# Stick-breaking attention: who copies the meta-token weights and the second half of the split keys

## The chip, the cores and the metric

The kernel runs on one core of a Trainium2 chip. The metric is the device time of one execution in microseconds (us), lower is better; a profile of a single execution of the kernel before the change stands beside it. The engines are called PE (TensorE matmul), PEld (its weight load), DVE (VectorE), ACT (ScalarE), POOL (GpSimd) and SP (SyncE, which here issues nearly all DMAs).

## The reference, cut to what matters

One layer of a decoder trunk: a normalised input goes through one wide projection into gated retention (4 heads) and stick-breaking attention (16 heads of 64), both are gated, merged, projected, and followed by a SwiGLU FFN. 512 tokens have 16 learned meta tokens put before them, so a row of keys is 528 long. The change lies in the attention alone:

```python
z = jnp.einsum('bhtd,bhsd->bhts', q_blk, k_pre) * scale
valid = (s_pos[None, :] < t_pos[:, None]) & (s_pos[None, :] >= PAD)
log_not = jnp.where(valid, jax.nn.log_sigmoid(-z), 0.0)
after = lax.cumsum(log_not, axis=3, reverse=True) - log_not
a = jnp.where(valid, jnp.exp(jax.nn.log_sigmoid(z) + after), 0.0)
outs.append(jnp.einsum('bhts,bhse->bhte', a, v_pre))
```

The weight of key s for token t is the sigmoid of the score times the product of the complementary sigmoids of all later keys. The first 16 of the 528 columns of the weights `a` belong to the meta tokens.

## The kernel before, in words

All operands of matmuls are split: a value is kept as a hi part, rounded to the matmul's type (fp32r), and a lo part, the rest. Three matmuls (hi by hi, hi by lo, lo by hi) stand for one product. `split` (line 99) makes the hi part on ACT (`activation(..., Copy)`) and the lo part on DVE (`lo_of`, line 96: a subtraction). Weights come from device memory through `load_units` (DMA at line 107 into one of two buffers `raw`, then `split` into `wh` and `wl`, five buffers each).

**The attention stage** works on 8 pairs of heads (two heads of 64 rows fill 128 partitions). For each pair:

- `qk_work` adds two pieces of work for the *next* pair: `q_steps` and `k_steps`. The score matmul contracts over 128 rows: for head 0 the query operand `qa` holds the hi rows above the lo rows, and the key operand `ka` holds the hi rows of k twice, rows 0:64 and again 64:128, so that one matmul gives hi by hi and lo by hi. Head 1 has the mirror image in `qb` and `kb`. A second matmul adds the key's lo part (`kl0`, `kl1`, with zeros in the unused half). `k_steps` makes the keys in two halves of 264 columns; for each half four ACT copies (lines 523 to 526) read the PSUM bank `pk`: `ka` hi, `ka` again into the other rows, `kb` hi, `kb` again; then two DVE subtractions (`kl`, line 96) make the lo parts and release the bank. There are two such banks (`bank_p`), which the projections of the stage share.
- `score` (line 594): two matmuls into a two-bank PSUM tile, two sigmoids on ACT (lines 616 and 618), a reversed running product on DVE (`sm`, line 620) and a product on DVE (`sp`, line 621) give the weights of one head and one block of 128 tokens.
- `turn_meta` (line 624): the 16 meta columns of the four blocks of a head have to be turned, so that keys lie on partitions. POOL copies each block's 16 columns with rounding (hi part, line 629), POOL subtracts (lo part, line 630), DVE transposes the 128x128 tile in 32x32 blocks into `x` (line 631), and four POOL copies (line 634) move the four groups of 32 rows of `x` into 32 rows of one tile, `am`: head 0 in rows 0:32, head 1 in rows 32:64. The whole tile is called `both`.
- `turn` (line 636): PE transposes the other columns into PSUM (`pb`, line 93), `split` makes `ah` and `al`.
- `values` (line 646): the output of a head; the first of its matmuls takes `both` (`pb<-am,vm`), the others `ah` and `al`. ACT (line 655) and DVE (line 656) take the result out of PSUM into `ysb`. The matmul with `both` reads the rows of both heads; those of the other head meet zero weights.

**Order.** `pair` writes out by hand in which order these are called: scores of head 0, a part of the transposes, scores of head 1 in between, `tm` (`turn_meta`) of head 0 at place 10, `pv` (`values`) of head 0 at place 13, `tm` of head 1 at place 17, `pv` of head 1 at place 19, the last. Between the calls `merge` puts matmuls of the projections (next pair's q and k, values, gates) by hand-set shares. In this stage the PE's order is pinned to that program order (`keep_in_program_order`). The orders of ACT, DVE, POOL and SP are mostly chosen when the program is built, by a scheduler that simulates a timeline; the POOL work of `Tokens.row_steps` (line 170, sums of token quarters, six steps behind each `tm` of pairs 1 to 5) is pinned as well. Each engine then runs its queue strictly in order, and so does SP with the DMAs it issues. `k_steps` of a pair is followed in the PE's order by a gate's or the values' projection before the next pair begins; only the first pair's keys are made directly ahead of it.

Tiles that matter here: `ka` one buffer, `kb` two, `mg` (the tile that is transposed) one, `x` one (shared with the values' tail), `am` one, the PSUM banks `bank_p` two and `bank_b` two.

Of the kernel before, what the change touches and what calls it, by code (L numbers as in the profile page):

```python
# [10 lines left out]
F32 = mybir.dt.float32  # L11
F32R = mybir.dt.float32r
AF = mybir.ActivationFunctionType
# [4 lines left out]
NM = 16  # L18
# [16 lines left out]
def hybrid_block(  # L35
# [18 lines left out]
    nc = tc.nc  # L54
    x, out = x[0], out[0]
# [9 lines left out]
    def bank_p():  # L65
        return ps_p.tile([P, 512], F32, tag="p", name="pp")
# [28 lines left out]
    def lo_of(lo, src, hi):  # L95
        nc.vector.tensor_tensor(lo, src, hi.bitcast(F32), op=ALU.subtract)  # L96
# [19 lines left out]
    def feat_units(src, kn=KD):  # L116

        cn = src.shape[1]
        return load_units(src, kn, cn, [(0, kn, c, P) for c in range(0, cn, P)])
# [269 lines left out]
    def feat_steps(dst, unit, xh, xl, kn=KD):  # L389
        wh, wl = unit  # L390
        for k in range(kn):
            mm(dst, wh[:, k, :], xh(k), start=(k == 0), stop=False)
            mm(dst, wh[:, k, :], xl(k), start=False, stop=False)
            mm(dst, wl[:, k, :], xh(k), start=False, stop=(k == kn - 1))
            yield 3 * xh(k).shape[-1]
# [12 lines left out]
    with tc.tile_pool(name="s2", bufs=2, side=RS, reuse_waits="tile") as s2:  # L408
# [88 lines left out]
        def qk_work(work, p):  # L497
            def q_load():
                return feat_units(w_in[:, O_SQ + P * p : O_SQ + P * (p + 1)])

            def q_steps(us):
                ps = bank_p()
                yield from feat_steps(ps, us[0], xtok, ltok)
                qa = s2.tile([P, T], F32R, tag="qa", name="qa", bufs=1)
                qb = s2.tile([P, T], F32R, tag="qb", name="qb")
                nc.scalar.activation(qa[0:64], ps[0:64], AF.Copy)
                nc.scalar.activation(qb[64:128], ps[64:128], AF.Copy)
                lo_of(qa[64:128], ps[0:64], qa[0:64])
                lo_of(qb[0:64], ps[64:128], qb[64:128])
                qks[p] = [(qa, qb)]  # L510

            def k_load():
                return feat_units(w_in[:, O_SK + P * p : O_SK + P * (p + 1)])

            def k_steps(us):
                ka = s2.tile([P, 2, 264], F32R, tag="ka", name="ka", bufs=1)
                kb = s2.tile([P, 2, 264], F32R, tag="kb", name="kb")
                kl1 = kl1s[p % 2]
                for i in range(2):
                    cs = slice(264 * i, 264 * (i + 1))  # L520
                    pk = bank_p()[:, :264]
                    yield from feat_steps(pk, us[0], lambda k: hT[:, k, cs], lambda k: hL[:, k, cs])
                    nc.scalar.activation(ka[0:64, i], pk[0:64], AF.Copy)
                    nc.scalar.activation(ka[64:128, i], pk[0:64], AF.Copy)
                    nc.scalar.activation(kb[64:128, i], pk[64:128], AF.Copy)
                    nc.scalar.activation(kb[0:64, i], pk[64:128], AF.Copy)
                    lo_of(kl0[0:64, i], pk[0:64], ka[0:64, i])
                    lo_of(kl1[64:128, i], pk[64:128], kb[64:128, i])
                qks[p] += [(flat(ka), flat(kb)), (flat(kl0), flat(kl1))]

            work.add(q_load, q_steps)
            work.add(k_load, k_steps)

        s3_pool = []
# [89 lines left out]
        def turn_meta(hd, att):  # L624

            g = s2.tile([P, NT, 32], F32R, tag="mg", name="mg", bufs=1)
            x = s2.tile([P, NT, 32], F32, tag="vs", name="x", bufs=1)
            for i in range(NT):
                nc.gpsimd.tensor_copy(g[:, i, 0:NM], att[i][:, 0:NM])  # L629
                nc.gpsimd.tensor_tensor(g[:, i, NM:], att[i][:, 0:NM], g[:, i, 0:NM].bitcast(F32), op=ALU.subtract)  # L630
            nc.vector.transpose(x.rearrange("p a b -> p (a b)"), g.rearrange("p a b -> p (a b)").bitcast(F32))
            am = ams[hd].rearrange("p (i b r) -> p i b r", i=NT, b=4)
            for b in range(4):
                nc.gpsimd.tensor_copy(am[:, :, b, :], x[32 * b : 32 * (b + 1)])

        def turn(j, att):
            w = T - j * P
# [26 lines left out]
        def pair(p):  # L664
# [9 lines left out]
            def tm(hd, j):  # L674
                turn_meta(hd, att[hd])

                if 1 <= p < 6:
                    for _ in range(6):
                        next(token_sums, None)
# [623 lines left out]
```

## Time and profile before

| | us |
|---|---|
| median of 3 runs | 1223.07 (1222.41 to 1224.04) |
| the profiled execution | 1223.93 |
| its span | 1222.2 |
| PE busy in the span | 1173.2 |
| DVE, ACT, POOL busy | 875.8, 534.0, 381.2 |
| start to 59 us (input norm, values, first q and k): PE busy | 48.70 of 59 |
| 59 to 300 us (the pairs): PE, DVE, ACT, POOL busy | 221.45, 203.06, 154.02, 142.41 of 241 |
| 300 us to the end (retention, output projection, FFN): PE busy | 903.08 of 922 |

How to read it: PE is nearly always busy, and matmul ends are modelled, so what can be won without fewer matmuls is the time in which PE waits. A group's row names the line, the engine, the operation, output and input tiles, the number of instructions, their busy time and the mean of one in ns, then the idle time of the engine before them and what ended it. A line of the view of waits names the engine and line that waited, what it waited for, the total, the number of times and the longest. Timeline rows start with the start and the duration in us. The granted TensorE clock was 1.00 in the pairs' stage. DMA rows give the time from issue to landing.

### The profile page before, as it was taken

To read this page: it belongs to the slowest core of one execution; us is meant where nothing else is said; L and a number is where in the kernel's file an instruction comes from. 1 tells how busy PE (TensorE), PEld (TensorE's weight loads), DVE (VectorE), ACT (ScalarE), POOL (GpSimd) and SP (SyncE) were. 2 spreads that over 40 slices of the span, in tenths; PEclk is the share of its full clock that TensorE was granted. 3 is DMA by queue.
4 is the path that set the end of the run, shared out by engine and by line. 5 is a ranking of instruction groups with operands and counts; after the bars stand their busy time and mean duration, and the time that the engine had idled before them with its cause. 6 is when DMAs were issued, how large, how long until landed. Compare 5 with 4: busy or idle time off the path is not lost.

```text
span 1222.2 us, 18904 instructions
## 1 busy us (share of the span) xinstructions
PE 1173.2 (96%) x7629; PEld 1064.6 (87%) x7629; DVE 875.8 (72%) x1138; ACT 534.0 (44%) x873; POOL 381.2 (31%) x422
## 2 busy tenths in 40 slices
PE   7999998889999999989999999999999999999997
PEld 6888888788889988988898889778899999998886
DVE  6588888887537885586678747776889999984333
ACT  5476666655424434333332424334464444443221
POOL 2037767554033220230213030000256666630000
PEclk9999999999999999999999999999999999999999
DMA  6331111114643214122421424424223333343211
GB/s 192 87 95 44 53 52 56 49 44 144 222 139 110 70 45 137 35 80 71 134 70 45 138 69 121 143 107 155 70 70 105 104 104 104 105 163 130 85 53 69
DMA packets 94503, 118.25 MB, mean 97 GB/s; under 512 B 2488, under 2 KB 71104, under 8 KB 94416
## 3 DMA queue, kind: packets, MB, share of 16 engines
q1 hardware_dynamic: 93984, 115.98, 29.0%
q8 instruction: 60, 0.98, 0.3%
q10 hardware_dynamic: 432, 1.07, 0.3%
q14 instruction: 27, 0.22, 0.1%
HBM read 109.96 MB, written 7.08 MB: 96 GB/s over the span
## 4 chain that ended last, share of the span: by engine, by line
PE 74%; DVE 12%; ACT 3%; POOL 2%; DMA 2%; issue 2%; DVEq 0%; POOLq 0%; ACTq 0%; SPq 0%
PE pp L90 31%; PE pb L90 20%; PE pa L90 18%; PE pc L90 4%; DVE wl L96 2%; DVE sm L620 2%; PE pb L93 2%; DVE sp L621 2%; DVE sl L96 1%; ACT wh L99 1%; POOL mg L629 1%; DMA raw<-in_w_in_dram 1%; DVE kl L96 1%; DMA raw<-in_w_sb_out_dram 1%; POOL mg L630 1%
## 5 line engine op out<-in xcount | busy, mean ns | idle before, releaser
L96 DVE TENSOR_TENSOR wl<-raw,wh 128x1024 fp32r<-128x1024 f32 (+1 forms) x202 | 274.0, 1365 | 81.3 <-ACT wh L99 78.1
L99 ACT ACTIVATE wh<-raw 128x1024 fp32r<-128x1024 f32 (+1 forms) x202 | 201.4, 1007 | 261.3 <-PE pa L90 85.5
L90 PE MATMUL pp<-hT,wh 128*128 128x512 f32 (+2 forms) x308 | 108.7, 353 | 12.9 <-DVE qb L96 7.9
L90 PE MATMUL pp<-hL,wh 128*128 128x512 f32 (+2 forms) x308 | 103.5, 336 | 0.0
L90 PE MATMUL pp<-hT,wl 128*128 128x512 f32 (+2 forms) x308 | 103.4, 336 | 0.0
L96 DVE TENSOR_TENSOR wl<-st,wh 128x1024 fp32r<-128x1024 f32 x54 | 81.0, 1505 | 9.5 <-ACT wh L99 9.5
L90 PE MATMUL pp<-qk,wh 128*128 128x512 f32 x256 | 83.2, 399 | 2.0 <-ACT qk L99 1.7
L90 PE MATMUL pp<-wh,hT 128*128 128x256 f32 (+1 forms) x240 | 77.1, 322 | 2.5 <-DVE kl L96 1.8
L90 PE MATMUL pp<-wh,hL 128*128 128x256 f32 (+1 forms) x240 | 75.3, 314 | 0.8 <-DVE ss L142 0.8
L90 PEld LDWEIGHTS pp<-hT,wh 128*128 128x128 f32 x308 | 58.1, 189 | 20.2 <-issue 9.0
L90 PE MATMUL pp<-wl,hT 128*128 128x256 f32 (+1 forms) x240 | 75.1, 313 | 0.0
L99 ACT ACTIVATE wh<-st 128x1024 fp32r<-128x1024 f32 x54 | 56.0, 1055 | 35.5 <-POOL st L254 17.1
L252 POOL TENSOR_TENSOR st<-raw 128x1024 f32<-128x1024 f32 x7 | 17.2, 2461 | 166.8 <-DMA raw<-in_w_in_dram 166.8
L143 POOL TENSOR_TENSOR rs<-rs,nhalf 128x1 f32<-128x1 f32 x20 | 12.7, 634 | 181.2 <-DVE rs L142 181.2
L629 POOL CAST mg<-sp 128x16 fp32r<-128x16 f32 x64 | 31.1, 487 | 109.5 <-DVE sp L621 53.6
L90 PEld LDWEIGHTS pp<-hT,wl 128*128 128x128 f32 x308 | 58.0, 188 | 6.2
L90 PE MATMUL pa<-hL,wh 128*128 128x264 f32 (+1 forms) x192 | 61.6, 321 | 0.0
L620 DVE TENSOR_TENSOR_SCAN sm<-sm,mask 128x528 f32<-128x528 f32 (+1 forms) x64 | 59.7, 945 | 2.6 <-ACT sm L616 2.2
L90 PE MATMUL pa<-hT,wl 128*128 128x264 f32 (+1 forms) x192 | 61.6, 321 | 0.0
L90 PE MATMUL pa<-hT,wh 128*128 128x264 f32 (+1 forms) x192 | 61.6, 321 | 0.0
L90 PEld LDWEIGHTS pp<-hL,wh 128*128 128x128 f32 x308 | 58.2, 189 | 3.8
L90 PEld LDWEIGHTS pp<-qk,wh 128*128 128x128 f32 x256 | 47.6, 188 | 13.4 <-ACT qk L99 2.4
(334 smaller groups left out, 3847.7 us busy)
## 6 DMA issues: line engine op xcount, KB each, us to landing
raw<-in_w_in_dram SPq DMA_DIRECT2D x31, 1024.0 KB, 5.1
raw<-in_w_ffn_in_dram SPq DMA_DIRECT2D x22, 1024.0 KB, 5.1
raw<-in_w_in_dram SPq DMA_DIRECT2D x26, 512.0 KB, 4.1
raw<-in_w_ffn_out_dram SPq DMA_DIRECT2D x11, 1024.0 KB, 4.9
raw<-in_w_ret_out_dram SPq DMA_DIRECT2D x8, 1024.0 KB, 4.9
raw<-in_w_sb_out_dram SPq DMA_DIRECT2D x4, 1024.0 KB, 7.5
raw<-in_w_out_dram SPq DMA_DIRECT2D x4, 1024.0 KB, 5.1
ysb<-in_x_dram SPq DMA_DIRECT2D x4, 512.0 KB, 9.0
```

What stands on the lines that cost most here:

```text
L90: return keep(nc.tensor.matmul(*args, **kw))
L93: return keep(nc.tensor.transpose(dst, src, idn))
L96: nc.vector.tensor_tensor(lo, src, hi.bitcast(F32), op=ALU.subtract)
L99: ins = nc.scalar.activation(hi, src, AF.Copy)
L143: nc.gpsimd.tensor_tensor(dst, dst, nhalf[:n], op=ALU.pow)
L252: nc.gpsimd.tensor_tensor(y, A11, A21, op=ALU.subtract)
L620: nc.vector.tensor_tensor_scan(rev, rev, mask[:, r0:][:, ::-1], 0.0, op0=ALU.mult, op1=ALU.max)
L621: nc.vector.tensor_tensor(sp, sp, sm[:, r0 + 1 : L + 1], op=ALU.mult)
L629: nc.gpsimd.tensor_copy(g[:, i, 0:NM], att[i][:, 0:NM])
L630: nc.gpsimd.tensor_tensor(g[:, i, NM:], att[i][:, 0:NM], g[:, i, 0:NM].bitcast(F32), op=ALU.subtract)
```

## The change

In `k_steps` ACT makes one hi copy of each key half per head instead of two; after both halves, one DMA for `ka` and one for `kb`, issued by SP, copy the 64 rows with 528 columns into the other 64 rows. In `turn_meta` the hi part is made by ACT instead of POOL; the subtraction stays on POOL and the transpose on DVE; the four moves of 32 rows into `am` become four DMAs issued by SP instead of POOL copies. There are 16 calls of `turn_meta` and 8 of `k_steps`.

```diff
                     nc.scalar.activation(ka[0:64, i], pk[0:64], AF.Copy)
-                    nc.scalar.activation(ka[64:128, i], pk[0:64], AF.Copy)
                     nc.scalar.activation(kb[64:128, i], pk[64:128], AF.Copy)
-                    nc.scalar.activation(kb[0:64, i], pk[64:128], AF.Copy)
                     lo_of(kl0[0:64, i], pk[0:64], ka[0:64, i])
                     lo_of(kl1[64:128, i], pk[64:128], kb[64:128, i])
+                nc.sync.dma_start(ka[64:128].bitcast(F32), ka[0:64].bitcast(F32))
+                nc.sync.dma_start(kb[0:64].bitcast(F32), kb[64:128].bitcast(F32))
                 qks[p] += [(flat(ka), flat(kb)), (flat(kl0), flat(kl1))]
...
             for i in range(NT):
-                nc.gpsimd.tensor_copy(g[:, i, 0:NM], att[i][:, 0:NM])
+                nc.scalar.activation(g[:, i, 0:NM], att[i][:, 0:NM], AF.Copy)
                 nc.gpsimd.tensor_tensor(g[:, i, NM:], att[i][:, 0:NM], g[:, i, 0:NM].bitcast(F32), op=ALU.subtract)
             nc.vector.transpose(x.rearrange("p a b -> p (a b)"), g.rearrange("p a b -> p (a b)").bitcast(F32))
             am = ams[hd].rearrange("p (i b r) -> p i b r", i=NT, b=4)
             for b in range(4):
-                nc.gpsimd.tensor_copy(am[:, :, b, :], x[32 * b : 32 * (b + 1)])
+                nc.sync.dma_start(am[:, :, b, :].bitcast(F32), x[32 * b : 32 * (b + 1)])
```

## The prediction

> **What bounds the kernel now.** I read the page's list of engines first, then the busy times by stretch (start, the pairs of heads, the rest), because the change touches only the pairs.
>
> ```profile
> PE 1173.2 (96%) x7629; PEld 1064.6 (87%) x7629; DVE 875.8 (72%) x1138; ACT 534.0 (44%) x873; POOL 381.2 (31%) x422
> ...
> 59.00:300.00 241.00, 221.45 (x1505) 201.45 (x1506) 203.06 (x320) 154.02 (x336) 142.41 (x260) 1.00 0.22 67
> ```
>
> PE is busy 96% of the span; in the pairs' stage 221.45 of 241.00 us. The change takes no matmul away, so what it can win is the 19.55 us in which PE idles there; what it can lose is not bounded by that. DVE comes next with 203.06 (84%), ACT has 87 us free, POOL 99. So POOL's own load bounds nothing. Whom PE waits for, in the view of waits of the same stretch:
>
> ```profile
> PE pp L90 <- DVE qb L96: 6.9, 7, 1.8
> PE pp L90 <- DVE kl L96: 5.2, 6, 1.4
> PE pb L93 <- DVE ysb L656: 3.1, 4, 1.3
> PE pb L93 <- DVE al L96: 2.0, 2, 1.1
> ```
>
> These four lines are 17.2 of the 19.55 us, and all name DVE: PE waits until DVE has read a PSUM bank. The change takes nothing off DVE's list of instructions. It can help only by making DVE wait less, and for POOL DVE waits little (first row):
>
> ```profile
> DVE x L631 <- POOL mg L630: 4.0, 10, 0.6
> ...
> ACT sm L616 <- DVE sp L621: 8.1, 8, 2.4
> ```
>
> **The change, part by part.** First the loads it moves, by groups of instructions:
>
> ```profile
> L629 POOL CAST mg<-sp 128x16 fp32r<-128x16 f32 x64 | 31.1, 487 | 109.5 <-DVE sp L621 53.6 <-PE pa L90 45.8 <-ACT wh L99 9.9
> L634 POOL CAST am<-x 32x128 fp32r<-32x128 f32 x64 | 28.6, 446 | 10.6 <-DVE x L631 8.0 <-PE pa L90 0.5
> ...
> L526 ACT ACTIVATE kb<-pp 64x264 fp32r<-64x264 f32 x16 | 6.2, 388 | 0.2
> L524 ACT ACTIVATE ka<-pp 64x264 fp32r<-64x264 f32 x16 | 6.1, 382 | 0.2
> ...
> L99 ACT ACTIVATE sh<-tm 128x512 fp32r<-128x512 f32 x4 | 2.5, 615 | 0.0
> ...
> L99 ACT ACTIVATE sh<-tm 128x128 fp32r<-128x128 f32 x4 | 1.2, 311 | 4.8 <-DVE tm L953 4.8
> ```
>
> POOL loses 31.1 + 28.6 = 59.7 us, 5% of the span, on an engine that limits nothing: worth 0 by itself. ACT loses 6.2 + 6.1 = 12.3 us. It gains 64 copies of 128x16 from SBUF, which the trace does not show. Between the two rows of such copies an element costs (615 - 311)/384 = 0.79 ns, so 16 elements cost about 311 - 112 x 0.79 = 222 ns, and 64 of them 14.2 us. Net ACT load: +1.9 us, under ACT's 87 idle us: 0, and 1.9 if that cover were gone.
>
> *Keys, the ACT side.* Four ACT copies per half become two. Where DVE's `kl` waits for the last of them, it starts two copies earlier. The first pair shows it (ACT and DVE in the timeline, PE's next matmul in the chain of waits):
>
> ```profile
> 57.50 0.39 ACT L526 ACTIVATE kb<-pp 64x264 fp32r<-64x264 f32 x1
> ...
> 57.92 0.42 DVE L96 TENSOR_TENSOR kl<-pp,ka 64x264 fp32r<-64x264 f32 x1 [0.39 <-ACT kb L526]
> ...
> 58.94 3.02 PE pp L90 x12
> ```
>
> DVE idled 0.39 us for ACT there and PE began behind it at 58.94. Two copies are 0.77 us, but DVE has only 0.39 to give: gain 0.4. In the pairs' stage proper `kl` starts late because DVE is busy with other work. I take 0.4 (from 0 to the 5.2 us of the `kl` line).
>
> *Keys, the DMA side.* Two DMAs of 132 KB a pair. The nearest rows of a price are a 256 KB store and the weight loads (KB each, us from issue to landing):
>
> ```profile
> gb_d<-go SPq DMA_DIRECT2D x4, 256.0 KB, 2.1
> ...
> raw<-in_w_in_dram SPq DMA_DIRECT2D x26, 512.0 KB, 4.1
> raw<-in_w_in_dram SPq DMA_DIRECT2D x31, 1024.0 KB, 5.1
> ```
>
> So about 2.1 us from issue, at most 5.1 + 2.1 behind a 1 MB load. Behind a pair's keys the PE's order has a whole projection for a gate or the values, 24 matmuls or more, before the next pair's first score: hidden, 0. The first pair has no such cover, but its last key copy would end near 57.1, its DMAs land by 59.6, and the first score comes after the 3.02 us of projection above, at 61.96. That leaves 2.4 us; behind one 512 KB load issued at the same time (4.1) it would still be 0.8 ahead. 0.
>
> *Meta weights, hi parts.* DVE's transpose waits for POOL's last subtraction. One turn in the timelines of DVE and POOL:
>
> ```profile
> 105.24 1.21 DVE L96 TENSOR_TENSOR wl<-raw,wh 128x1024 fp32r<-128x1024 f32 x1
> 106.84 0.31 DVE L631 STREAM_TRANSPOSE x<-mg 128x128 f32<-128x128 f32 x1 [0.39 <-POOL mg L630]
> ...
> 105.38 1.13 POOL L629 CAST mg<-sp 128x16 fp32r<-128x16 f32 x1 [0.23 <-DVE sp L621]
> 106.59 0.22 POOL L630 TENSOR_TENSOR mg<-sp,mg 128x16 fp32r<-128x16 f32 x1
> ```
>
> Read plainly, a 1.13 us cast becomes a 0.22 us ACT copy and `x` is ready 0.9 us earlier. But the cast ends 0.06 us after DVE's `wl`, which has two SBUF inputs, and the subtraction then takes 0.22: the 1.13 looks like time spent locked out, and a subtraction that began at 105.7 would sit there in the cast's place until 106.5. Then `x` starts about 0.2 us earlier, not 0.9, and DVE, busy until 106.45, could have used 0.39 at most. [...]
>
> Over the stage DVE waits 4.0 us for POOL here, and PE sees a part through `ysb`, which is queued behind `x` (3.1 us). I take half of 0.2/0.39 of 4.0, because DVE's gain reaches PE only where PE waits: 1.0, between 0 and 4.0. Against it: ACT now waits for `sp` with `ah`, `sm` and `ysb` of the same queue behind it, and for them wait DVE and then PE. Nearest row: ACT waits 1.0 us a time for `sp` today (8.1 over 8). If each of the 16 turns did that, ACT would lose 16 of its 87 idle us; I take 0.3 for PE and 2.0 as the end, the whole of today's `al` line again.
>
> *Meta weights, the moves.* Each turn now issues four DMAs behind `x`. They pass through SP's in-order queue, together with the weight loads that wait there for a free buffer. Three turns of head 1, each with SP's last load, the transpose, and the matmul that needs the rows:
>
> ```profile
> 79.50 0.37 SPq L107 DMA_DIRECT2D raw<-in_w_in_dram  x1
> 81.83 0.29 DVE L631 STREAM_TRANSPOSE x<-mg 128x128 f32<-128x128 f32 x1
> 85.19 0.40 PE L90 MATMUL pb<-am,vm 128*128 128x512 f32 x1
> ...
> 133.97 0.37 SPq L107 DMA_DIRECT2D raw<-in_w_in_dram  x1
> 134.33 0.31 DVE L631 STREAM_TRANSPOSE x<-mg 128x128 f32<-128x128 f32 x1 [0.39 <-POOL mg L630]
> 139.70 0.42 PE L90 MATMUL pb<-am,vm 128*128 128x512 f32 x1
> ...
> 252.43 0.37 SPq L217 DMA_DIRECT2D raw<-in_w_in_dram  x1
> 252.76 0.31 DVE L631 STREAM_TRANSPOSE x<-mg 128x128 f32<-128x128 f32 x1 [0.39 <-POOL mg L630]
> 258.42 0.40 PE L90 MATMUL pb<-am,vm 128*128 128x512 f32 x1
> ...
> 122.70 0.31 DVE L631 STREAM_TRANSPOSE x<-mg 128x128 f32<-128x128 f32 x1
> 132.17 0.39 PE L90 MATMUL pb<-am,vm 128*128 128x512 f32 x1
> ```
>
> With an idle ring: 0.15 to start, three issues of 0.37, then 2.1 for the last: about 3.4 us after `x` ends. The matmul comes 3.1 us after `x` in the first of these turns, 5.1 and 5.4 in the next two, and 9.2 in the last, which belongs to head 0 and is typical of it. So 0.3 us is lost in the first and nothing elsewhere. But a 1 MB load has been issued just ahead in all three turns of head 1 (256 columns of 1024 rows); it lands 5.1 us later, at 84.6, 139.1 and 257.5. If the small transfers drain with or right behind it, they still arrive by 85.5, 139.4 and 257.8. I take 0.3 in all; the end is the rival below. A load behind the four issues is held by 1.5 us. ACT, the first to read a load, waits for one only twice in the stage, so I take 0 for that, and the 3.2 us of this row again as the end:
>
> ```profile
> ACT wh L99 <- DMA raw<-in_w_in_dram: 3.2, 2, 3.0
> ```
>
>
> *Sum.* Gains 0.4 + 1.0 = 1.4; costs 0.3 + 0.3 = 0.6; net -0.8 on the profiled execution's 1223.93 (span 1222.2 and 1.7 around it): 1223.1. That execution lies 0.86 above the median of 1223.07, so 1222.3 in the median's terms. About 0.2%, 2.45 us, is what a measurement of this kernel can tell from no change; my sum is a third of it.
>
> **Rivals.** *The rows come late (slower).* Place: the first matmul of `values`, whose position on PE is fixed. If the small DMAs wait until the load ahead has landed and only then need their own 2.1 us, they arrive at 86.7, 141.2 and 259.6: late by 1.5, 1.5 and 1.2, together 4.2. Less the 1.4 of gains and with ACT's 0.3 that is +3.1; a head-1 turn or two more of the same kind make +4.1, so 1227.2. It decides from a total lateness of about 3.6 us. For it: the loads do stand just ahead of `x`, in the same queue. Against it: a landing is counted from issue and most of the small DMAs' 2.1 us can pass while the load still drains. [...]
>
> *DVE gains all that POOL cost it (faster).* All 4.0 us of DVE's waits for POOL and 0.8 in the keys reach PE: -4.8, 1218.3. For it: DVE is 84% busy and every PE wait above is on DVE. Against it: the subtraction stays on POOL, so the wait has the same releaser, now with one more engine in the chain.
>
> *Another order.* The build-time scheduler sees other durations and may queue ACT, DVE and SP differently (a load that waits for its buffer ahead of a turn's four moves, for one); the 19.55 idle us of PE can move by some us either way.
>
> **How the numbers follow.** Forecast 0.50; rows late 0.18; DVE freed 0.22; another order 0.10, of it 0.04 faster and 0.06 slower. Hence faster than 0.2%: 0.26; within: 0.50; slower: 0.24. The likeliest case's own range is 1220.6 to 1225.5. The 8-in-10 range takes in both rivals' times: 1218.0 to 1228.0.
>
> **What would show it.** Right: PE's idle time in the pairs' stage still 18 to 21 us; POOL near 82 us busy there; ACT near 156; the 128x16 ACT copies at 0.2 to 0.25 us; `x` still released by POOL; no wait of PE on a DMA of `am` beyond the first pair. Wrong towards slower: PE or PEld lines that wait for DMA `am` with over 3 us in total, or ACT waits for `sp` well above 8 us with more PE waits on `al`. Wrong towards faster: the DVE line for POOL gone and the `ysb`, `kl` and `qb` lines of PE shorter by over 3 us.

## The result, and the profile after

The changed kernel takes 1234.35 us in the median of four runs (1230.12 to 1236.21), the kernel before 1223.26 beside it: ratio 1.0081 (95% interval 1.0065 to 1.0097), 0.8% or some 10 us slower. The profiled execution took 1235.95 us with a span of 1234.2. Ratios and intervals, here and below, leave out executions in a slower state; the medians of two runs hold one such execution each (the moves by DMA and the kernel before, both with the reversed loop).

The busy times of the pairs' stage after (columns as before: PE, PEld, DVE, ACT, POOL, granted clock, DMA share, GB/s):

```profile
59.00:300.00 241.00, 214.31 (x1414) 193.94 (x1414) 202.38 (x307) 144.71 (x359) 94.19 (x131) 0.98 0.25 70
```

POOL is relieved as intended, from 142.41 to 94.19 us. PE idles 26.69 us in this stretch instead of 19.55, and the granted clock is 0.98 instead of 1.00. The order of PE's matmuls is the same in both kernels, so each can be matched with its twin: PE is behind by 3.4 us where the kernel before stands at 100 us, by 7.7 at 150, 12.3 at 250, and 13.7 at 304.7, the end of the pairs; at the last matmul it is 12.0. So the loss arises in the pairs.

Whom PE waits for in the changed kernel. This and every later view of PE's waits is taken from 55 to 325 us, so that the whole stage lies in it for every kernel; in the kernel before `qb` has 7.9 us there (6.9 from 59 to 300), `kl` 5.2, `ysb` 3.1 and `al` 2.9.

```profile
PE pp L90 <- DVE qb L96: 12.5, 7, 2.7
PE pb L90 <- DMA am<-x: 3.6, 4, 1.5
PE pb L93 <- DVE al L96: 3.5, 3, 1.9
PE pp L90 <- DVE kl L96: 2.9, 4, 1.0
PE pb L93 <- DVE ysb L656: 2.8, 4, 1.1
...
PE pa L90 <- DMA ka<-ka: 1.2, 1, 1.2
```

Two kinds of wait are new: 3.6 us for the moved rows and 1.2 for the keys. The largest growth is at a place that the change doesn't touch: `qb`, the lo part of the next pair's queries on DVE, from 7.9 to 12.5. What DVE and ACT wait for in the stage:

```profile
ACT mg L629 <- DVE sp L621: 31.1, 34, 2.7
...
DVE x L631 <- POOL mg L630: 0.3, 1, 0.3
```

DVE hardly waits for POOL any more (4.0 before), and still it is late. Its two-input instructions in the scores, the scan and the product, have become slower, the same 64 of each: first the kernel before, then the changed one (busy us, mean ns).

```profile
L620 DVE TENSOR_TENSOR_SCAN sm<-sm,mask 128x528 f32<-128x528 f32 (+1 forms) x64 | 59.7, 945 | 2.6 <-ACT sm L616 2.2
L621 DVE TENSOR_TENSOR sp<-sp,sm 128x528 f32<-128x528 f32 (+1 forms) x64 | 38.4, 613 | 1.9
```

```profile
L620 DVE TENSOR_TENSOR_SCAN sm<-sm,mask 128x528 f32<-128x528 f32 (+1 forms) x64 | 63.6, 1005 | 3.7 <-ACT sm L616 3.3
L621 DVE TENSOR_TENSOR sp<-sp,sm 128x528 f32<-128x528 f32 (+1 forms) x64 | 42.4, 672 | 2.8
```

Together that is 106.0 us instead of 98.1.

One turn shows why. It is that of head 0 in the second pair, from the timelines of POOL, DVE and PE, before:

```profile
91.62 0.51 POOL L630 TENSOR_TENSOR mg<-sp,mg 128x16 fp32r<-128x16 f32 x1
...
94.75 0.22 POOL L630 TENSOR_TENSOR mg<-sp,mg 128x16 fp32r<-128x16 f32 x1
95.45 2.56 POOL L634 CAST am<-x 32x128 fp32r<-32x128 f32 x4 [0.48 <-DVE x L631]
98.09 0.73 POOL L170 TENSOR_TENSOR go<-hT 128x256 f32<-128x256 f32 x1
...
95.01 0.31 DVE L631 STREAM_TRANSPOSE x<-mg 128x128 f32<-128x128 f32 x1 [0.33 <-POOL mg L630]
...
99.08 0.36 PE L90 MATMUL pp<-hT,wh 128*128 128x264 f32 x1 [0.58 <-DVE qb L96]
```

And after:

```profile
93.26 0.73 POOL L630 TENSOR_TENSOR mg<-sp,mg 128x16 fp32r<-128x16 f32 x1 [10.69 <-ACT mg L629]
93.94 0.73 POOL L170 TENSOR_TENSOR go<-hT 128x256 f32<-128x256 f32 x1
...
95.53 0.56 POOL L630 TENSOR_TENSOR mg<-sp,mg 128x16 fp32r<-128x16 f32 x2
96.05 0.85 POOL L170 TENSOR_TENSOR go<-go 128x256 f32<-128x256 f32 x1
96.86 1.69 POOL L170 TENSOR_TENSOR go<-hT 128x256 f32<-128x256 f32 x1
98.51 0.69 POOL L630 TENSOR_TENSOR mg<-sp,mg 128x16 fp32r<-128x16 f32 x1
...
96.22 1.79 DVE L620 TENSOR_TENSOR_SCAN sm<-sm,mask 128x528 f32<-128x528 f32 x1
...
99.23 0.31 DVE L631 STREAM_TRANSPOSE x<-mg 128x128 f32<-128x128 f32 x1
...
102.52 0.36 PE L90 MATMUL pp<-hT,wh 128*128 128x264 f32 x1 [2.18 <-DVE qb L96]
```

The token sums (line 170) are the difference. Before, POOL begins them at 98.09, behind the turn's four moves. After, it begins them at 93.94, between the turn's first and second subtraction. From the first subtraction to the transpose it takes 3.4 us before (91.62 to 95.01) and 6.0 after. The DVE scan of 528 columns took 1.24 us in this turn before. Now it takes 1.79: it begins while one token sum runs (96.05 to 96.90), and the next sum, which starts beside it, takes 1.69 us and ends 0.5 us after it. Over the whole changed kernel the products of 528 columns that overlap a token sum in time take 0.98 us on average (4 of them), the others 0.69 (12); in the kernel before none of them overlaps one. DVE's queue behind it, `x`, `wl`, `qa`, `qb`, is late, and PE stands still for 2.18 us instead of 0.58.

The cause is in the code, as these timelines and the runs below bear out. A token sum is pinned: it stays behind the POOL instruction that the program writes before it; POOL's other instructions are placed by the build-time scheduler. With the moves on POOL, that instruction was the fourth move, the last of the turn. With the moves on SP it is the subtraction of block 3, whose weights (528 columns) DVE finishes *first* of the four. So the sums are let in behind the earliest of the turn's subtractions and the others queue among them.

### The profile page after: what moved, and what is told of

Its sections match the earlier page's. It is cut to its first block, busy times and chain, and to the rows that moved or that the text cites. A ratio compares the mean times of both kernels' runs of the same rounds, so it can differ in the third digit from the quotient of the medians.

```text
span 1234.2 us, 18957 instructions
## 1 busy us (share of the span) xinstructions
PE 1178.5 (95%) x7629; PEld 1068.6 (87%) x7629; DVE 883.9 (72%) x1138; ACT 531.1 (43%) x905; POOL 334.5 (27%) x294
## 4 chain that ended last, share of the span: by engine, by line
PE 76%; DVE 11%; DMA 3%; issue 3%; ACT 3%; POOL 2%; SPq 1%; DVEq 0%; POOLq 0%; ACTq 0%
PE pp L90 32%; PE pb L90 20%; PE pa L90 17%; PE pc L90 4%; DVE sm L620 3%; DVE wl L96 2%; PE pb L93 2%; DVE sl L96 1%; ACT wh L99 1%; DVE sp L621 1%; POOL go L170 1%; DMA ysb<-in_x_dram 1%; DMA am<-x 1%; DMA raw<-in_w_in_dram 1%; POOL mg L630 1%
## 5 line engine op out<-in xcount | busy, mean ns | idle before, releaser
L90 PE MATMUL pp<-hT,wh 128*128 128x512 f32 (+2 forms) x308 | 110.7, 359 | 16.0 <-DVE qb L96 12.5
L630 POOL TENSOR_TENSOR mg<-sp,mg 128x16 fp32r<-128x16 f32 x64 | 28.4, 446 | 177.1 <-ACT mg L629 177.0
L620 DVE TENSOR_TENSOR_SCAN sm<-sm,mask 128x528 f32<-128x528 f32 (+1 forms) x64 | 63.6, 1005 | 3.7 <-ACT sm L616 3.3
```

The costliest lines, as they stand in the source:

```text
L90: return keep(nc.tensor.matmul(*args, **kw))
L620: nc.vector.tensor_tensor_scan(rev, rev, mask[:, r0:][:, ::-1], 0.0, op0=ALU.mult, op1=ALU.max)
```

## The experiments

The ratio is always to the kernel before, run beside it on the same chip.

**The parts one by one.** The theories were three: ScalarE's hi copies hold up its queue (A); any change of timing reshuffles the schedule (B); the moves by DMA are the loss (C).

*Only the hi parts on ACT* (line 629 of the change):

> Only the meta weights' hi copies move from GpSimd to ScalarE; moves and keys stay as before. Theory A: this is the larger part, because ScalarE stood 31 us waiting for the products sp of the scores with these copies at the head of its queue; 1227 to 1231 us, with PE's waits for DVE qb near 12 us instead of 6.9 and waits of ScalarE's mg copies for sp over 20 us. Rival C (the moves by DMA are the cause, the ScalarE copies are hidden in its 87 idle us): 1221 to 1225 us.

Measured: 1219.22 us, ratio 0.9960 (0.9944 to 0.9975): faster, and below the range of C too. A falls. ACT waits long for `sp` here too (26.7 us), and of PE's waits the one that grew most is that for `al`, from 2.9 to 3.7 us. Some of what PE waits for:

```profile
PE pp L90 <- DVE kl L96: 4.9, 6, 1.1
PE pp L90 <- DVE qb L96: 4.9, 6, 1.8
...
PE pb L93 <- DVE ysb L656: 0.2, 1, 0.2
```

The waits for `qb` fell from 7.9 to 4.9 and those for `ysb` from 3.1 to 0.2; DVE waits no longer for POOL at `x`.

*Only the keys' DMAs* (lines 523 to 528 of the change):

> Only the keys' second copy is a DMA; the meta weights stay as before. Theory A (the hi copies on ScalarE stall its queue, and the four moves come late): the keys cost little. In the changed kernel the first pair's score waited 1.2 us for this DMA and the keys' bank was released earlier elsewhere, so 1221 to 1225 us, same as before. Rival B (any small change reshuffles the order that the scheduler builds, and that alone costs the 11 us): this one is slower by several us as well, 1227 or more.

Measured: 1223.45 us, ratio 0.9997 (0.9987 to 1.0006): no difference. B falls with it, at least as a cause that any edit would set off.

*Only the moves by DMA* (line 634 of the change):

> Only the four moves of a turn become DMAs; hi copies stay on GpSimd, keys as before. Theory A: PE waits for these rows 3 to 6 us in total (3.6 us in the changed kernel), so 1226 to 1229 us. Rival C: nearly the whole loss, 1231 to 1235 us. A third reading, that the rows are late only because ScalarE made the hi copies late: 1222 to 1225 us.

Measured: 1231.13 us, ratio 1.0061 (1.0046 to 1.0076). C was right as to the part. But PE waits hardly at all for `am` here:

```profile
PE pp L90 <- DVE qb L96: 14.6, 8, 3.0
...
PE pb L90 <- DMA am<-x: 0.5, 1, 0.5
```

The loss is in the moves' part, and it isn't PE waiting for late rows.

*Hi parts and keys, moves left on POOL*:

> The change without the DMA moves: hi copies on ScalarE and keys by DMA, moves by GpSimd as before. Theory A: the changed kernel less the lateness of the rows, 1228 to 1231 us. Rival C: 1221 to 1225 us.

Measured: 1218.53 us, ratio 0.9959 (0.9945 to 0.9974). The change without its moves beats both kernels, and both forecasts were too slow.

**Place or path.** New theory E: the moves on POOL anchored the token sums, and what costs is that the sums now run earlier. Rival F: the path by DMA costs (issue, landing, the queue behind the weight loads).

*The kernel before, moves on POOL, with the sums written ahead of the moves*, no DMA (the edit shortened: the sums are also taken out from behind `turn_meta`):

```diff
                 nc.gpsimd.tensor_tensor(g[:, i, NM:], att[i][:, 0:NM], g[:, i, 0:NM].bitcast(F32), op=ALU.subtract)
+            mid()      # the six token sums of this turn, until now behind the moves
             nc.vector.transpose(...)
```

> The kernel before, no DMA added and nothing moved to ScalarE; only the six steps of token sums on GpSimd are traced behind the turn's subtractions and ahead of its transpose and moves, so that their pin no longer hangs on the last move. Theory E (the moves' place in the program was the anchor that kept the long GpSimd sums behind a turn's chain; without it they run between the subtractions and lock VectorE out): slower by 4 to 10 us, 1228 to 1234, with VectorE's scans and products 6 to 9 us longer in total and PE's waits for DVE qb over 10 us. Rival F (the DMA path is the cost: issue of 0.60 us each, landing, ring order): no change, 1222 to 1225.

Measured: 1229.62 us, ratio 1.0043 (1.0027 to 1.0059). With nothing moved to a DMA at all, a loss appears, half as large and with the same sign, PE's wait for `qb`. That line, and the same turn as above from the timelines (line numbers behind the edit are one higher):

```profile
PE pp L90 <- DVE qb L96: 13.8, 7, 3.0
...
91.44 0.51 POOL L630 TENSOR_TENSOR mg<-sp,mg 128x16 fp32r<-128x16 f32 x1
91.92 0.74 POOL L170 TENSOR_TENSOR go<-hT 128x256 f32<-128x256 f32 x1
...
99.41 0.31 DVE L632 STREAM_TRANSPOSE x<-mg 128x128 f32<-128x128 f32 x1 [0.98 <-POOL mg L630]
...
101.29 0.36 PE L90 MATMUL pp<-hT,wh 128*128 128x264 f32 x1 [2.98 <-DVE qb L96]
```

From first subtraction to transpose 8.0 us, as in the kernel with the moves alone by DMA (94.19 to 102.16). DVE's scans and products take 105.3 us, 7.2 more than before, within E's 6 to 9.

*Moves by DMA, blocks in reversed order*, so that the subtraction written last is the one that becomes ready last:

```diff
-            for i in range(NT):
+            for i in reversed(range(NT)):
```

> The four moves by DMA alone, as in the run of that part, but the loop over the four blocks runs backwards, so that the subtraction traced last is the one whose input comes last and the token sums stay behind all four. Theory E: back to 1222 to 1226 us, as VectorE's scans and products lose their 8 us of excess. Rival F: 1230 to 1232 as with the loop forwards.

Measured: 1220.92 us, ratio 0.9967 (0.9955 to 0.9979), against 1.0061 without the reversal: F falls, and the time is below E's range as well. In the same turn the sums stand behind all four subtractions again, and from the first subtraction to the transpose it takes 3.4 us as before:

```profile
94.27 0.52 POOL L630 TENSOR_TENSOR mg<-sp,mg 128x16 fp32r<-128x16 f32 x1
...
97.40 0.22 POOL L630 TENSOR_TENSOR mg<-sp,mg 128x16 fp32r<-128x16 f32 x1
97.58 0.75 POOL L170 TENSOR_TENSOR go<-hT 128x256 f32<-128x256 f32 x1
...
97.66 0.31 DVE L631 STREAM_TRANSPOSE x<-mg 128x128 f32<-128x128 f32 x1 [0.33 <-POOL mg L630]
```

PE's wait for `qb` fell from 14.6 to 10.2 us only, not to the 7.9 of before; how the time can be below that of before all the same is told in the last section.

*The whole change with the reversed loop*:

> The whole change with the loop over the blocks backwards. Theory E: the loss by order goes, the rows' own lateness (3.6 us of PE's waits for the DMAs of am) stays against the gain of the hi copies: 1220 to 1225 us. Rival F: 1232 to 1236 as the changed kernel.

Measured: 1222.58 us, ratio 0.9982 (0.9971 to 0.9993): a one-word edit takes back 1.0081 - 0.9982 = 1.0%, 12 us.

*Hi parts alone with the reversed loop*, as a control:

> Hi copies on ScalarE, moves and keys as before, loop backwards. A control: the moves still anchor the sums here, so theory E expects no more than 1 to 2 us against the forward loop's 1219.2, either way; if the backward loop by itself is worth several us in this kernel too, it is not the anchor that it mends.

Measured: 1219.83 us, ratio 0.9960 (0.9945 to 0.9975), as without the reversal. Where the moves anchor the sums, the block order is worth nothing.

**The controls, and what the path costs.** G: the reversal is worth something by itself.

*The kernel before with the reversed loop*:

> The kernel before with the four blocks of a turn handled in reversed order, and nothing else: the moves stay on POOL, so the token sums are still pinned behind the last move. Theory E (the sums' place in POOL's queue is what costs): no change, ratio 0.998 to 1.002, PE's wait for qb within 1.5 us of the 7.9 of before. Rival G (the reversed order is itself worth something, so that the runs with it proved less than I read from them): 2 to 4 us faster, ratio 0.997 to 0.998 or below, as in the run with the moves by DMA and the reversed loop.

Measured: 1225.16 us, ratio 1.0001 (0.9992 to 1.0010), `qb` 8.0. G falls.

*The change with the reversed loop and the moves on POOL*:

> The whole change with the reversed loop, but with the four moves back on POOL. It differs from the changed kernel with the reversed loop (1222.58) by the moves' path alone. Theory E: the DMA path still costs something by itself, about the 2.6 us that PE waited for am there, plus up to 1 us in the first turns; so 1218 to 1220, ratio 0.995 to 0.997, and like hi part plus keys without the reversal (1218.53). Rival F (the DMA path costs nothing once the sums are in place): 1222 to 1223, and the hi part's gain is lost for another reason.

Measured: 1218.88 us, ratio 0.9953 (0.9940 to 0.9967). Against the whole change with the reversed loop (0.9982), the path by DMA costs 0.3%, 3.5 us.

*The changed kernel with its DMAs issued by POOL*:

```diff
-                nc.sync.dma_start(am[:, :, b, :].bitcast(F32), x[32 * b : 32 * (b + 1)])
+                nc.gpsimd.dma_start(am[:, :, b, :].bitcast(F32), x[32 * b : 32 * (b + 1)])
```

> The changed kernel with the four moves still by DMA but issued by POOL instead of SP: POOL's traced order again ends each turn with the moves, so the token sums come behind them, and the moves' queue holds no weight loads. Theory E: the loss goes, 1219 to 1224, ratio 0.996 to 1.001, PE's wait for qb at 9 us or less and DVE's products back to the mean of before; the issue on POOL can cost up to 2 us of that. Rival F (small DMAs are late whatever queue they are in): 1228 or more, PE waits for am over 3 us. Against both: if POOL needs over 1 us for an issue, four of them delay the next turn's subtractions, the gain ends near 0.

Measured: 1249.74 us, ratio 1.0210 (1.0195 to 1.0225): the worst of all. By its numbers F's forecast held (1228 or more, over 3 us for `am`); E's time missed by 26 us, though the wait for `qb` fell to 4.6 us and DVE's products took 37.7 us against 38.4 before, as E says. As a test between the two it is inconclusive, because the moves are later than on SP. What PE (55 to 325 us) and POOL (59 to 300 us) wait for:

```profile
PE pb L90 <- DMA am<-x: 12.9, 6, 3.4
...
POOL am L634 <- issue: 16.7, 18, 2.7
POOL am L634 <- PE pb L93: 9.6, 6, 1.9
```

POOL stands at the first move until PE has released `am`, and needs 0.55 us of its own for each issue (31.1 us for 56 in the stage). It also stands idle before them for 16.7 us, in 18 pieces, for which the profile shows no reason; on SP, in the changed kernel, the first move of 14 turns out of 16 starts 0.06 to 0.07 us behind the end of `x`. SP stands 88.2 us at the moves there until `x` is ready (15 times), but its queue has only DMA issues behind them. DVE's scans took 69.4 us here, 9.7 more than before; why was not looked into. Half-clock stretches (last section) fill 27.3 us of this kernel's pairs, so up to 13.7 us of its loss are theirs.

*The changed kernel, with four POOL copies into a tile that nobody reads* behind the four DMAs; it adds work and has no other purpose than the anchor:

```diff
                 nc.sync.dma_start(am[:, :, b, :].bitcast(F32), x[32 * b : 32 * (b + 1)])
+                nc.gpsimd.tensor_copy(spare, x[32 * b : 32 * (b + 1)])
```

> The changed kernel, with its DMAs, in its own block order, and added work alone: behind the four DMAs of a turn, POOL copies the same four groups of 32 rows of x into a small tile that nothing reads. Its only use is that POOL's traced order again ends each turn behind x, so that the token sums are pinned there, as before. Theory E (the sums' place in POOL's queue): the loss goes although POOL works some 25 us more than in the changed kernel; PE's wait for qb at 8 us or less (12.5 in the changed kernel), PE still waits 2 to 4 us for am, 1219 to 1223 in all, ratio 0.996 to 0.9995. If it comes to about 1222, as with the reversed loop, the moves' DMA path costs the 3 to 4 us that are still open; if to 1219, they were the sums that begin one step earlier. Rival F (the DMA path is the loss): 1231 to 1236, as the changed kernel or worse.

Measured: 1224.30 us, ratio 0.9999 (0.9988 to 1.0009). With 24.2 us more of useless work on POOL the changed kernel is 0.8%, some 10 us, *faster*. This is the plainest test of E, since it adds nothing but the anchor. PE's waits:

```profile
PE pp L90 <- DVE qb L96: 4.8, 7, 1.7
PE pb L90 <- DMA am<-x: 4.5, 5, 1.2
```

The time is 1.3 us above E's range: the path by DMA costs more here than I had put in (0.9999 - 0.9959 = 0.4%, 4.9 us, against hi parts and keys alone).

DVE's scans and products (lines 620 and 621) show the same split. They take 105.3 to 106.5 us in the three kernels in which the sums stand among the subtractions of head 0 (sums first, the changed kernel, the moves alone), and 95.9 to 98.7 us with the reversed loop or the useless copies, against 98.1 before.

**The account**, in ratios to the kernel before, 1 in 1000 being 1.22 us. By the run with the useless copies (0.9959, 0.9999, 1.0081): hi parts and keys -5.0 us, the path of the moves +4.9, the lost anchor +10.0. By the runs with the reversed loop (0.9953, 0.9982, 1.0081): -5.7, +3.5, +12.1. Each of the two sums gives the measured +9.9 by construction, since its terms are steps from one run to the next; what speaks for the account is that the two ways agree within some 2 us, which is how uncertain each term is. Read at the end of the pairs instead, from one profile each, the terms are -2.7, +6.6, +9.8 and -3.5, +6.1, +11.1, of 13.7 us.

These prices hold for this kernel and don't simply add elsewhere. Without any DMA the lost anchor cost 5.2 us. Without the hi parts on ACT the moves by DMA with the reversed loop are 4.2 us *faster* than the kernel before with it (0.9967 against 1.0001), though 2.1 us behind it at the end of the pairs.

## Why the prediction was wrong, point by point

*POOL loses 59.7 us, "worth 0 by itself".* This is the step that failed. The load did come off (48 us in the window), and load bounds nothing, as I said. But one of the instructions taken off was a place in POOL's order: the pinned token sums stood behind the fourth move. I listed what the moves pass through on SP, their new queue, and didn't ask what stood behind them on POOL, their old one, though `row_steps` is told above as pinned, six steps behind each `tm`. Price in this kernel: 10 to 12 us, the whole loss.

*"Another order"* was the rival nearest to it, with "some us either way" and a chance of 0.10. It was neither a mechanism nor priced, and it spoke of ACT, DVE and SP, not of POOL.

*Hi parts: gain 1.0 less 0.3.* The direction was right and the size was not: 4.7 us in the medians; in the profile the lead is 3.5 us at the end of the pairs. It came about as the rival "DVE gains all that POOL cost it" had it (4.0 of DVE's waits gone, -4.8 priced with the keys). I had halved the gain twice, because a subtraction that begins earlier could still be locked out by DVE's `wl`. With the cast gone, `x` simply found its data there. What I had read from one turn holds for the casts of the kernel before: those that overlap a scan, a product or a `wl` of DVE took 0.60 us on average (46 of them), the others 0.20 (18). But it priced the wrong step: what DVE loses time to here are the sums, not the casts (the scan that took 1.79 us beside token sums instead of 1.24, the products at 0.98 instead of 0.69 us). The copy itself was priced well: 222 ns estimated, and

```profile
L629 ACT ACTIVATE mg<-sp 128x16 fp32r<-128x16 f32 x63 | 13.6, 216 | 33.0 <-DVE sp L621 31.1 <-DVE x L631 1.4
```

*ACT's new waits for `sp`, 0.3, at most 2.0.* The waits are far longer than I took, 31.1 us against 16, and cost nothing that shows: ACT has the slack. My sign "ACT waits for `sp` well above 8 us" was a false alarm; it needed its second half, more waits on `al`, and those grew by 0.6 us only, with a new one of 0.7 at another matmul.

*Keys, ACT side 0.4, DMA side 0.* Together -0.4 us (-1.6 to +0.7) in the run of the keys alone, as forecast. But the cover of the first pair was miscounted: I took 57.1 for the end of the last key copy, and that was the first half's. The second half stands behind another weight split on ACT; in the kernel before its copies run from 59.17 to 60.76. After (ACT, PE):

```profile
59.25 0.39 ACT L523 ACTIVATE ka<-pp 64x264 fp32r<-64x264 f32 x1
...
63.08 0.36 PE L90 MATMUL pa<-ka,qa 128*128 128x264 f32 x1 [1.24 <-DMA ka<-ka]
```

The DMA is issued at 59.66, and the score waits 1.24 us for its keys. With the keys alone it waits 0.7, and `kl` falls from 5.2 to 4.4: the forecast of 0 came out although one of its steps was wrong, which is luck.

*The moves, 0.3.* Too small in the changed kernel: PE waits 3.6 us for `am`, at four turns; with the moves alone by DMA it waits 0.5. Two terms were mis-sized. An issue takes 0.60 us, not 0.37 (its median below), so that even with nothing ahead of them the last of four lands 3 x 0.60 + 1.9 us behind the first issue; in the usual turn it lands 3.8 to 3.9 us behind the end of `x`, not 3.4. The 0.15 us to start were an estimate, close to the 0.13 of POOL's move in the kernel before (95.45, `x` ending at 95.32), and no run shows them for a DMA: the first move starts 0.06 us behind `x`. And behind a load the moves landed only after it: in seven turns of the changed kernel the first of them came 0.15 to 0.17 us behind the load.

```profile
L634 SPq DMA_DIRECT2D am<-x x64: 585/599/1625, 74.2 to 315.4; - x64
```

The turn with the longest wait, from the timelines of SP, DVE and PE:

```profile
141.00 0.55 SPq L107 DMA_DIRECT2D raw<-in_w_in_dram  x1
141.65 2.62 SPq L634 DMA_DIRECT2D am<-x  x4
...
141.08 0.31 DVE L631 STREAM_TRANSPOSE x<-mg 128x128 f32<-128x128 f32 x1
...
147.37 0.47 PE L90 MATMUL pb<-am,vm 128*128 128x512 f32 x1 [1.53 <-DMA am<-x]
```

The load lands 5.4 us after its issue, at 146.4; the moves land between 146.6 and 147.2, 4.9 to 3.5 us after theirs instead of the usual 1.9. So my reading "they drain with or right behind it" was right, and the rival's place too; its total of 4.2 us came out nearly right by luck, with another working: not 2.1 us behind the load, but 0.2 to 0.8, at a slower issue.

*Signs.* PE idle 18 to 21 us: 26.7. POOL near 82: 94.2; a subtraction takes 445 ns on average there instead of 381, and the 56 token sums 51.9 us instead of 43.6. ACT near 156: 144.7, in a stretch with 91 matmuls fewer. `x` released by POOL: once, for 0.3 us. DMA waits for `am` over 3 us: the sign towards slower came, and with 3.6 us it stood for about a third of the loss at most.

**What stays open.** How much of the 3.5 to 4.9 us of the moves' path is landing (PE's 2.6 to 4.5 us for `am`) and how much comes from the sums that begin one step earlier than behind POOL copies was not separated. Nor was a part of the anchor's loss: sums written first, without a DMA, cost 5.2 us, and the moves alone by DMA with their lost anchor 11.5 (1.0061 against 0.9967). From first subtraction to transpose the first two turns of head 0 with token sums take 8.0 and 8.5 us in both; those of head 1 take 7.8 and 5.8 with the sums written first, 9.7 and 8.7 with the moves by DMA. Half-clock stretches, below, are part of that difference: the pairs have four with the moves alone, two with the sums first.

## What to carry to other kernels

An instruction on an engine with slack can still be worth microseconds by its place, 10 to 12 here: before moving it, list what is ordered behind it in its *old* queue, what that would then stand in front of, and what of it makes instructions of the bound engine longer when both run at once (here DVE's products, 0.98 us beside a token sum and 0.69 otherwise). When a change has several parts, run each alone: here the gain (-5.0 us, hi parts and keys, moves left on POOL: 1218.53 us) and the loss were in different parts, and the sum hid both. A new long wait on an engine with slack (ACT's 31.1 us for `sp`) is no finding until somebody behind it waits as well.

## What the runs showed of the hardware

**A gap of PE cost more than its length here, depending on where it fell.** The changed kernel, in stretches of 3.41 us (PE busy is the first busy column; granted clock is the third column from the right):

```profile
125.82:129.23 3.41, 3.41 (x29) 3.33 (x27) 3.26 (x5) 3.28 (x9) 3.41 (x5) 1.00 0.00 0
129.24:132.65 3.41, 1.19 (x11) 1.09 (x9) 3.33 (x5) 1.97 (x6) 3.33 (x5) 1.00 0.16 27
132.65:136.06 3.41, 3.41 (x18) 3.41 (x17) 3.37 (x7) 0.81 (x2) 3.25 (x5) 0.50 0.56 154
136.06:139.47 3.41, 3.41 (x27) 3.27 (x26) 3.18 (x5) 2.48 (x6) 0.82 (x2) 1.00 0.00 0
```

PE idled for 2.22 us of one stretch; in the next the granted clock was 0.50, and a PE that was busy throughout did 18 matmuls where the full stretches around it have 29 and 27. In the traces of the changed kernel and of the kernel before, these half-clock stretches last 3.41 us each (the one at the end of PE's work apart) and begin a multiple of 3.41 us apart: 132.65, 163.37 and 255.53 in the changed kernel are 9 and 27 such steps apart. So by my estimate each costs up to half its length, 1.7 us, and these three up to 5.1 of the 13.7 us. The idle times narrow the condition. In the changed kernel the six stretches ahead of a half-clock one had 1.90 to 2.65 us idle, in the kernel before the three had 2.25 to 3.15. From 17 us on, where the record of the clock begins, the other stretches on that grid had at most 1.81 us idle in these two traces (190.67 in the changed kernel). The edge is not sharp: in the other runs a few stretches from 1.68 us on were followed by half clock, and one with 1.84 us (the whole change with the reversed loop) was not. The 2.18 us gap at 102.52, shown above, was spread over two stretches (1.59 in the first) and was followed by no half clock. A stretch a little over half idle (1.90 of 3.41 us) was enough.

The profiled executions differ in such stretches after the pairs too, where nothing was changed: the kernel before has them at 433.37, 542.60 and 651.82 us, the hi parts alone only at 537.92, and the moves with the reversed loop only at 543.88. That kernel is 2.9 us behind the kernel before at the end of the pairs and 2.7 us ahead at the last matmul. The clock of its runs says the same: the mean granted clock of its six runs is 0.9962, that of the kernel before beside them 0.9938, which is worth some 2.9 us by my estimate (0.0024 x 1220). So where time is won or lost is read at the end of the changed stage, and how much from the medians of runs; of the 0.3% by which that kernel is ahead, the pairs' stage shows nothing.
